# Projection steps spread among the groups of recurrence products, by priority and by TensorE's queue order

## The chip, the cores and the metric

The kernel runs on one core of one Trainium2 chip. The metric is device time in microseconds (us) of one execution: the median of three runs before is 3184.94 us (3180.3 to 3184.98). Queries of the trace give times from the start of the profiled span. TensorE is called PE in them, its weight loads PEld, VectorE DVE, ScalarE ACT, GpSimd POOL, and the queue from which most transfers are issued SP.

## The reference

One layer of a transformer-like block on 1024 latent tokens and 256 context tokens, width 1024, everything in float32: a modulated SwiGLU, then a mixer, then a second SwiGLU and a norm. What matters here is the mixer:

```python
c_q, c_k, c_v, c_g, c_r, c_rk, c_rv, c_gret, c_grw = jnp.split(uc @ w_in, IN_SPLITS, axis=-1)
l_q, l_k, l_v, l_g, l_r, l_rk, l_rv, l_gret, l_grw = jnp.split(ul @ w_in, IN_SPLITS, axis=-1)
...
y_ret_l, _ = retention_segment(axial_rope(hd(l_q), rows, cols), axial_rope(hd(l_k), rows, cols) * k_scale,
                               hd(l_v), log_gamma, ret_state_c)
...
def step(s, inp):                      # rwkv7_scan, two directions, 8 heads of 64
    rt, wt, kt, vt, at, bt = inp
    sa = jnp.einsum('zbhvk,zbhk->zbhv', s, at)
    s_new = s * wt[..., None, :] + sa[..., :, None] * bt[..., None, :] + vt[..., :, None] * kt[..., None, :]
...
rw_out = rwkv_readout(y_rw, r, k, v, xg, g1, g2, r_k, ln_w, ln_b).astype(dt) @ w_rwkv_o
return (jax.nn.sigmoid(gate_ret) * ret_out + jax.nn.sigmoid(gate_rw) * rw_out) @ w_out
```

The recurrence (`rwkv7_scan`) needs only `r`, `k`, `v` and its decays. The columns of `w_in` for the retention (`q`, `k`, `v`, `g`) and for the two gates (`gret`, `grw`) are needed only after it.

## The kernel before, in words

The change lies in one stage, some 950 us long, in which two independent bodies of work share the engines.

*The recurrences* (`Rwkv.recurrences`) go through the tokens in 10 steps. A step takes one pair of 64-token chunks for each of the two directions (z = 0, 1). `prep` loads a pair's operands, scales them, and computes its Gram products `gps` on TensorE (64 rows deep), masked by VectorE into `g`; it also transposes (`btps`, `vtps`) and, for one direction, computes `bops`. `inverse` inverts the triangular parts of `g` in 32x32 blocks on VectorE (`invt`, `invx`, 60 instructions for both directions), with a transposition through DRAM before and after it (SP: `scr<-g`, `invn<-scr`, `scr<-invx`, `g<-scr`). `join` makes 64x64 inverses of the 32x32 ones with the small products `hps` and `xps`. `chain` then applies the pair to the state `S`, once for each chunk: `q` from the state, `q` from the values (`wv`), the correction `u`, the state's update (also named `u` in the trace) and, for latents, the outputs (again `q`). The products of `chain` are 64 by 64, except those from `S`. `readout` normalises finished tokens. `prep` and `inverse` of step s + 2 stand behind `chain` of step s in the program, and the ring of four buffers allows no more.

*The projections* (`Mixer.fill`: `qkvg`, then `gates`) are 72 blocks of 128 columns by up to 512 tokens. `block` splits the block's weights into a high and a low part (`K.cols`: SP loads `wraw`, ScalarE makes `whi`, GpSimd `wlo`) and runs 8 steps of three matmuls each (`mm3`, tile `fps`), 576 steps and 1728 matmuls in all. ScalarE evacuates the bank into `gs`, rotary turns follow for `q` and `k` (SP `rsw`, GpSimd and VectorE), and SP stores the result. Two banks, two weight buffers.

A scheduler orders each engine's queue at build time: it takes ready instructions by priority, which is the place in the program unless the program says otherwise, along its own estimate of time. `fill` is written after `recurrences`, so its instructions have the lowest priority and are put where the estimate has an engine free. On the chip each queue is then executed in that order. A float32 product of the recurrence stands once in the order and twice in the trace.

Of the kernel before, what the change touches and what calls it, by code (L numbers as in the profile page):

```python
# [17 lines left out]
P = 128  # L18
D = 1024
KT = 8  # L20
# [138 lines left out]
class Kern:  # L159
# [44 lines left out]
    def mm3(self, ps, w, ws, x, xs, start, stop, full=None):  # L204
        mm = self.nc.tensor.matmul
        xs = (full, xs) if full else xs
        mm(ps, w[0][:, ws], x[0][xs], start=start, stop=False)  # L207
        mm(ps, w[0][:, ws], x[1][xs], start=False, stop=False)  # L208
        mm(ps, w[1][:, ws], x[0][xs], start=False, stop=stop)  # L209

    def proj(self, ps, w, u, n):
# [315 lines left out]
class Mixer:  # L527
# [222 lines left out]
    def groups(self, which, u, here=False):  # L750

        for c0, n in which:
            for k in range(KT):
                for i in range(2):
                    if not here:
                        self.nc.sync.dma_start(out=u[i][:, k, :n].bitcast(F32), in_=self.dram["u", i][:, k, c0:c0 + n])
            yield c0, n, u
            here = False

    def block(self, u, n, col, pp):  # L760
        ps = pp.tile([P, 512], F32, tag="f", name="fps")[:, :n]
        self.K.proj(ps, self.K.cols(self.a["w_in"][0], col), u, n)
        return ps

    def qkvg(self, u, pool, pp):

        nc, a = self.nc, self.a
        for c0, n, u in self.groups(TURN, u, True):
            lat = c0 < TL
            if lat:  # L770
                cs = {}
                for k in ("cos", "sin"):
                    cs[k] = pool.tile([P, 512], F32, tag=k, name=k, bufs=1)
                    nc.sync.dma_start(out=cs[k], in_=a["cst_" + k][:, c0:c0 + n])
            for hd in range(4):
                for i, nm in enumerate(("q", "rk", "rv", "sg")):
                    if i in (0, 3) and not lat:
                        continue
                    ps = self.block(u, n, 512 * i + hd * P, pp)
                    t = pool.tile([P, 512], F32, tag="gs", name="gs")[:, :n]  # L780
                    if i == 3:
                        nc.scalar.activation(t, ps, AF.Tanh, scale=0.5)
                        nc.vector.scalar_tensor_tensor(out=t, in0=t, scalar=1.0, in1=ps, op0=ALU.add, op1=ALU.mult)
                    else:
                        nc.scalar.activation(t, ps, AF.Copy)
                    if i < 2 and lat:
                        sw = pool.tile([P, 512], F32, tag="rsw", name="rsw", bufs=1)
                        for b in range(0, P, 64):
                            nc.sync.dma_start(out=sw[b:b + 32], in_=t[b + 32:b + 64])
                            nc.sync.dma_start(out=sw[b + 32:b + 64], in_=t[b:b + 32])  # L790
                        nc.gpsimd.tensor_tensor(out=sw, in0=sw, in1=cs["sin"], op=ALU.mult)
                        nc.vector.tensor_tensor(out=t, in0=t, in1=cs["cos"], op=ALU.mult)
                        nc.vector.tensor_tensor(out=t, in0=t, in1=sw, op=ALU.add)
                    nc.sync.dma_start(out=self.dram[nm][hd, :, c0:c0 + n], in_=t)

    def gates(self, u, pool, pp):

        for c0, n, u in self.groups(LAT[::-1], u, True):
            for m0, nm in ((3584, "gret"), (4608, "grw")):
                for m in range(8):  # L800
                    ps = self.block(u, n, m0 + m * P, pp)
                    g = pool.tile([P, 512], F32, tag="gs", name="gs")
                    self.nc.scalar.activation(g, ps, AF.Tanh, scale=0.5)
                    self.nc.sync.dma_start(out=self.dram[nm][m, :, c0:c0 + n], in_=g)

# [45 lines left out]
class Rwkv(Mixer):  # L851
# [16 lines left out]
    def prep(self, s, z, ring, tmp, pp):  # L868
# [73 lines left out]
        bt = ring.tile([P, 4, 2, P], F32, tag="bt", name="bt")  # L942
        for h0 in range(0, 4, 2):
            ps = pp.tile([P, 2, 2, P], F32, tag="mm", name="btps")
# [4 lines left out]
        wv = ring.tile([P, 4, 2, P], F32, tag="wv", name="wv")  # L949
        ps = pp.tile([P, 4, P], F32, tag="mm", name="vtps")  # L950
        for hp in range(4):
# [39 lines left out]
    def join(self, g, tmp, pq):  # L991
# [3 lines left out]
        for e in range(2):  # L995
# [3 lines left out]
            psh, psx = (pq.tile([P, 8, 32], F32, tag="us", name=nm) for nm in ("hps", "xps"))  # L999
            nc.vector.transpose(tt[rf].rearrange("p q t -> p (q t)"), g[rf, e, :, :, rf].rearrange("p a b t -> p (a b) t"))  # L1000
            for q in range(8):
                nc.tensor.matmul(psh[rs, q], gb(rf, q, rs), tt[rf, q], start=True, stop=True, tile_position=(of, os))
            nc.scalar.activation(tt[rs], psh[rs], AF.Copy)
            for q in range(8):
                nc.tensor.matmul(psx[rf, q], tt[rs, q], gb(rs, q, rs), start=True, stop=True, tile_position=(os, of))
            nc.vector.tensor_copy(out=g[rf, e, :, :, rs].rearrange("p a b t -> p (a b) t"), in_=psx[rf])

    def chain(self, un, z, y, first, last, tmp, ps_):
# [8 lines left out]
        for e in (0, 1) if z == 0 else (1, 0):  # L1017
# [3 lines left out]
            for hp in range(4):  # L1021
                mm(q[qr, hp], ar[:, hp, e, ac], S[:, hp], start=hp == 0, stop=False)
            for hp, h in every:
# [4 lines left out]
            for hp, h in every:  # L1028
                mm(us[A, hp, hc[h]], g[A, e, hp, h, A], qa[A, hp, hc[h]], start=True, stop=True)
            nc.scalar.activation(wv[A, :, e], us[A], AF.Copy)  # L1030
            if not (last and e == 1 - z):
                st = us.rearrange("p h v -> p (h v)")[:, :256].rearrange("p (h v) -> p h v", h=4)
                for hp, h in every:
                    mm(st[hc[h], hp], bt[:, hp, e, hc[h]], wv[:, hp, e, hc[h]], start=True, stop=True)
                for h in range(2):
# [3 lines left out]
            if lat:  # L1039
                for hp, h in every:  # L1040
                    mm(q[R, hp, hc[h]], g[:, e, hp, h, R], wv[:, hp, e, hc[h]], start=False, stop=(hp, h) == (3, 1))
                if first:
                    nc.scalar.activation(y[R], f4(q[R]), AF.Copy)
                else:
                    nc.vector.tensor_tensor(out=y[R], in0=y[R], in1=f4(q[R]), op=ALU.add)
# [31 lines left out]
    def recurrences(self, ctx):  # L1077
# [14 lines left out]
        ready(1)  # L1092
        late, joined = [], set()

        def join(i):
# [456 lines left out]
```

## Time and profile before

| | |
|---|---|
| median of 3 runs | 3184.94 us |
| profiled execution | 3190.72 us, span 3188.8 us |
| TensorE busy | 2984.3 us (94%) |
| VectorE, ScalarE, GpSimd busy | 1891.5 (59%), 1041.9 (33%), 958.2 us (30%) |
| mean granted TensorE clock | 0.943 |
| projections (`fps`, L207 to L209), each of three lines | 576 matmuls, 236.4 to 240.6 us busy |

Busy time counts the time in which at least one instruction of an engine is in flight. Matmuls overlap, so their mean duration (some 420 ns for a projection matmul) is longer than the distance of their starts. "Granted clock" is the share of its full clock that TensorE was given; the page prints it in tenths for 40 slices of the span. The row of a stretch holds its borders, its length, then busy time and number of instructions of PE, PEld, DVE, ACT and POOL, then the granted clock, the share of the DMA engines and GB/s; when it is asked for one tile, engines without that tile may be missing.

### The profile page before, as it was taken

The page shows a single profiled execution, that of the slowest core. Times are in us where ns is not written, and L with a number is a line of the kernel's source. Part 1 is how long each engine was busy: PE and PEld are TensorE (multiplying, and loading weights), DVE is VectorE, ACT ScalarE, POOL GpSimd, SP SyncE. Part 2 cuts the span into 40 slices and gives each one's busy share as a digit, 9 for nine tenths or more (in the row PEclk, how much of TensorE's full clock was granted, in tenths as well). Part 3 has the DMA queues.
Part 4 walks back from the last instruction along what each step waited for, and adds up shares of the span by engine and source line. Part 5 has one row for each costly group of instructions (what it writes and reads, how often), then busy time and mean ns, then how long its engine had stood idle before and what let it go on. Part 6 is the DMA issues. An engine that isn't in the chain of part 4 may idle for free.

```text
span 3188.8 us, 45522 instructions
## 1 busy us (share of the span) xinstructions
PE 2984.3 (94%) x17239; PEld 2481.0 (78%) x17239; DVE 1891.5 (59%) x3226; ACT 1041.9 (33%) x1753; POOL 958.2 (30%) x768
## 2 busy tenths in 40 slices
PE   8999999999999999888888899897999799999998
PEld 4888888888887787677776777776778688888877
DVE  4886666544447783676656656754576777665012
ACT  5111111111114465433333334344424533332221
POOL 2111111111113411543333333332215433333542
PEclk9999999999999999887788799998999899999999
DMA  5433222111114446554544454544544344448641
GB/s 212 131 104 93 82 81 77 50 40 40 40 40 166 152 141 213 169 148 137 162 135 114 120 149 128 168 119 147 166 155 137 95 139 140 140 145 302 217 170 60
DMA packets 505747, 416.45 MB, mean 131 GB/s; under 512 B 93464, under 2 KB 402648, under 8 KB 505528
## 3 DMA queue, kind: packets, MB, share of 16 engines
q1 hardware_dynamic: 488976, 401.65, 40.9%
q10 hardware_dynamic: 16552, 11.90, 1.2%
q8 instruction: 136, 2.23, 0.3%
q14 instruction: 83, 0.68, 0.1%
HBM read 309.89 MB, written 99.35 MB: 128 GB/s over the span
## 4 chain that ended last, share of the span: by engine, by line
PE 69%; DVE 13%; DMA 8%; SPq 3%; issue 3%; ACT 2%; POOL 2%; DVEq 0%; ACTq 0%; POOLq 0%
PE psd L207 5%; PE psd L208 5%; PE psd L209 5%; PE p L208 4%; PE p L207 4%; PE p L209 4%; PE psg L209 3%; PE psu L207 3%; PE psu L208 3%; PE psu L209 3%; PE psg L208 3%; PE psg L207 3%; DVE invt L980 2%; DVE invx L981 2%; PE fps L209 1%
## 5 line engine op out<-in xcount | busy, mean ns | idle before, releaser
L197 POOL TENSOR_TENSOR wlo<-wraw,whi 128x512 fp32r<-128x512 f32 (+1 forms) x246 | 442.4, 1811 | 1281.2 <-ACT whi L196 1248.6
L389 DVE SCALAR_TENSOR_TENSOR h<-psd,g,h 128x512 f32<-128x512 f32 (+1 forms) x504 | 313.5, 656 | 272.4 <-PE psd L209 272.1
L196 ACT ACTIVATE whi<-wraw 128x512 fp32r<-128x512 f32 (+1 forms) x246 | 193.9, 804 | 328.9 <-DMA wraw<-in_w_in_dram 72.2
L207 PE MATMUL fps<-uh,whi 128*128 128x512 f32 (+1 forms) x576 | 240.6, 419 | 14.1 <-ACT whi L196 6.7
L207 PE MATMUL p<-v,fac 128*128 128x512 f32 x616 | 241.7, 393 | 11.4 <-ACT v L42 6.3
L209 PE MATMUL fps<-uh,wlo 128*128 128x512 f32 (+1 forms) x576 | 240.2, 418 | 7.5 <-POOL wlo L197 6.8
L208 PE MATMUL p<-v,fac 128*128 128x512 f32 x616 | 241.6, 392 | 4.6 <-DVE v L43 4.6
L209 PE MATMUL p<-v,fac 128*128 128x512 f32 x616 | 241.3, 392 | 0.0
L208 PE MATMUL fps<-ul,whi 128*128 128x512 f32 (+1 forms) x576 | 236.4, 411 | 2.9 <-DMA ul<-d_u 2.9
L207 PE MATMUL psd<-hh,whi 128*128 128x512 f32 (+1 forms) x528 | 189.7, 359 | 4.8 <-DVE h L389 4.6
L207 PE MATMUL psg<-uh,whi 128*128 128x512 f32 (+1 forms) x528 | 188.5, 357 | 0.9 <-ACT whi L196 0.9
L208 PE MATMUL psg<-ul,whi 128*128 128x512 f32 (+1 forms) x528 | 188.8, 358 | 0.4 <-POOL ul L259 0.4
L209 PE MATMUL psg<-uh,wlo 128*128 128x512 f32 (+1 forms) x528 | 188.7, 357 | 0.0
L207 PE MATMUL psu<-uh,whi 128*128 128x512 f32 (+1 forms) x528 | 187.9, 356 | 0.4 <-ACT whi L196 0.4
L208 PE MATMUL psu<-ul,whi 128*128 128x512 f32 (+1 forms) x528 | 187.8, 356 | 0.0
L209 PE MATMUL psu<-uh,wlo 128*128 128x512 f32 (+1 forms) x528 | 187.5, 355 | 0.0
L208 PE MATMUL psd<-hl,whi 128*128 128x512 f32 (+1 forms) x528 | 187.1, 354 | 0.0
L209 PE MATMUL psd<-hh,wlo 128*128 128x512 f32 (+1 forms) x528 | 186.7, 354 | 0.0
L376 ACT ACTIVATE hh<-sg 128x512 fp32r<-128x512 f32 (+1 forms) x66 | 36.9, 559 | 365.4 <-DVE sg L374 308.2
L43 POOL TENSOR_TENSOR fac<-draw,fac 128x512 fp32r<-128x512 f32 x88 | 114.4, 1305 | 138.6 <-ACT fac L42 135.7
L207 PEld LDWEIGHTS fps<-uh,whi 128*128 128x128 f32 x576 | 119.0, 207 | 40.4 <-ACT whi L196 8.9
L209 PEld LDWEIGHTS fps<-uh,wlo 128*128 128x128 f32 x576 | 118.8, 206 | 35.7 <-POOL wlo L197 10.4
(363 smaller groups left out, 7085.2 us busy)
## 6 DMA issues: line engine op xcount, KB each, us to landing
wraw<-in_w_in_dram SPq DMA_DIRECT2D x144, 256.0 KB
modw<-in_w_mod_dram SPq DMA_DIRECT2D x112, 256.0 KB
fraw<-in_ffn_w_gate_dram SPq DMA_DIRECT2D x88, 256.0 KB
hd<-d_hid SPq DMA_DIRECT2D x44, 512.0 KB
draw<-in_ffn_w_down_dram SPq DMA_DIRECT2D x88, 256.0 KB
wraw<-in_ffn_w_gate_dram SPq DMA_DIRECT2D x22, 512.0 KB
wraw<-in_ffn_w_up_dram SPq DMA_DIRECT2D x22, 512.0 KB
wraw<-in_ffn_w_down_dram SPq DMA_DIRECT2D x22, 512.0 KB
```

Of the source, the lines that this page charges most:

```text
L43: eng.tensor_tensor(out=v[1], in0=x, in1=v[0].bitcast(F32), op=ALU.subtract)
L196: nc.scalar.activation(hi[:, s], raw, AF.Copy)
L197: nc.gpsimd.tensor_tensor(out=lo[:, s], in0=raw, in1=hi[:, s].bitcast(F32), op=ALU.subtract)
L207: mm(ps, w[0][:, ws], x[0][xs], start=start, stop=False)
L208: mm(ps, w[0][:, ws], x[1][xs], start=False, stop=False)
L209: mm(ps, w[1][:, ws], x[0][xs], start=False, stop=stop)
L376: nc.scalar.activation(hh, s, AF.Copy)
L389: nc.vector.scalar_tensor_tensor(out=hs, in0=ps, scalar=gates()[v][:, m:m + 1], in1=hs, op0=ALU.mult, op1=ALU.add)
L980: eng.tensor_tensor(out=tv, in0=x[:, :, :m, i:i + 1].to_broadcast([P, 2, m, w]), in1=n[:, :, i:i + 1, i + 1:].to_broadcast([P, 2, m, w]), ...
L981: eng.tensor_tensor(out=x[:, :, :m, i + 1:], in0=x[:, :, :m, i + 1:], in1=tv, op=ALU.add)
```

## The change

While `recurrences` is traced, `mark` notes the priority at each group of recurrence products (and, in `chain`, the group's last product). Projection step j (a counter, 0 to 575) is then given the priority of a mark: the first one of the loop for j below 130, and the mark at the same share of the list for the rest. The block's weights get the priority of 16 steps earlier, reloads of tokens that of 8 steps earlier, and evacuation, rotary turn and store that of the step behind the block. From step 130 on, the first matmul of the three has to follow, in TensorE's queue alone, the linked recurrence product that is four links before its mark.

```diff
--- before.py
+++ after.py
     def mm3(self, ps, w, ws, x, xs, start, stop, full=None):
...
-        mm(ps, w[0][:, ws], x[0][xs], start=start, stop=False)
+        first = mm(ps, w[0][:, ws], x[0][xs], start=start, stop=False)
...
+        return first
...
+    FREE, SLACK, STEPS = 130, 4, 576
+
+    def mark(self, inst=None):
+        if inst is not None:
+            self.links.append(inst.ins.name if hasattr(inst, "ins") else inst.name)
+        self.marks.append((self.tc.cur_priority, len(self.links)))
+
+    def spot(self, ahead=0):
+        j = max(self.step - ahead - self.FREE, 0)
+        return self.marks[self.lead + min(j * (len(self.marks) - self.lead) // (self.STEPS - self.FREE), len(self.marks) - self.lead - 1)]
+
+    def at(self, ahead=0):
+        return self.tc.high_priority(offset=max(self.tc.cur_priority - self.spot(ahead)[0], 0))
+
     def block(self, u, n, col, pp):
         ps = pp.tile([P, 512], F32, tag="f", name="fps")[:, :n]
-        self.K.proj(ps, self.K.cols(self.a["w_in"][0], col), u, n)
+        with self.at(16):
+            w = self.K.cols(self.a["w_in"][0], col)
+        for k in range(KT):
+            with self.at():
+                x = self.K.mm3(ps, w, slice(k * P, (k + 1) * P), u, (slice(None), k, slice(0, n)), k == 0, k == KT - 1)
+            link = self.spot()[1] - 1 - self.SLACK
+            if self.step >= self.FREE and link >= 0:
+                x = getattr(x, "ins", x)
+                self.tc.add_manual_dep(x, self.links[link], mybir.DependencyInfo(mybir.DependencyClass.NoSync, mybir.DependencyReason.DATA), reason="in turn")
+            self.step += 1
         return ps
...
@@ qkvg, gates: evacuation, rotary turn and store of a block
+                    with self.at():
...
@@ groups: reload of the tokens
+                        with self.at(8):
...
@@ prep, join, chain: before each group of gps, btps, vtps, hps, xps
+            self.mark()
@@ chain: after each group of q, u, the state's update, the outputs
+            self.mark(x)
@@ recurrences
+        self.marks, self.links, self.step = [], [], 0
...
+        self.lead = len(self.marks)
```

Line numbers move by 1 to 40, those of the products named below by 30 to 37. In the order of TensorE's queue, at the third join (`hps`, `xps` of step 2) and the chain behind it (tile `btps` transposes for the next step), there stood before, without a projection matmul in between:

```order
L923 MATMUL gps<-ar,bk 128x128 x8
L1002 MATMUL hps<-tt,g 32x32 x8
L1005 MATMUL xps<-g,tt 32x32 x8
L1002 MATMUL hps<-tt,g 32x32 x8
L1005 MATMUL xps<-g,tt 32x32 x8
L1029 MATMUL u<-qa,g 64x64 x8
L1002 MATMUL hps<-tt,g 32x32 x8
L1034 MATMUL u<-wv,bt 64x64 x8
L923 MATMUL gps<-ar,bk 128x128 x4
```

In the new order the end of the same join and the products of the chain behind it stand so:

```order
L1039 MATMUL xps<-g,tt 32x32 x5
L978 MATMUL btps<-ident,bk 128x128 x8
L1039 MATMUL xps<-g,tt 32x32 x3
L1035 MATMUL hps<-tt,g 32x32 x8
L209 MATMUL fps<-uh,wlo 128x512
L1056 MATMUL q<-S_10082,ar 128x128 x2
L207 MATMUL fps<-uh,whi 128x512
L1059 MATMUL q<-wv,g 64x64
L208 MATMUL fps<-ul,whi 128x512
```

Single projection matmuls now stand between the products of the join and of the chain.

In the order of TensorE's queue in a later chain (first direction, from the state's products on), before:

```order
L1022 MATMUL q<-S_10081,ar 128x128
L1034 MATMUL u<-wv,bt 64x64 x8
L1041 MATMUL q<-wv,g 64x64 x8
L1022 MATMUL q<-S_10081,ar 128x128 x3
L1024 MATMUL q<-wv,g 64x64 x8
L207 MATMUL fps<-uh,whi 128x512
```

And in the new order, in a chain of the same direction:

```order
L1056 MATMUL q<-S_10081,ar 128x128 x4
L207 MATMUL fps<-uh,whi 128x512
L1059 MATMUL q<-wv,g 64x64
L208 MATMUL fps<-ul,whi 128x512
L1059 MATMUL q<-wv,g 64x64
L209 MATMUL fps<-uh,wlo 128x512
L1039 MATMUL xps<-g,tt 32x32 x8
```

The chain's own products, before in unbroken groups, are divided by single matmuls of the projections.

In SP's queue, where an inverse's result goes out to DRAM (`scr<-invx`) and comes back into `g`, there stood before:

```order
L987 DMA scr_13298<-invx 256x1x32 x4
L987 DMA scr_13312<-invx 256x1x32 x2
L989 DMA g<-scr_13298 32x8x32 x4
L987 DMA scr_13312<-invx 256x1x32 x2
L939 DMA d_bv_93<-in_r 128x4x128
L972 DMA scr_13855<-g 32x8x32
L989 DMA g<-scr_13312 32x8x32 x4
```

And now:

```order
L1019 DMA scr_13298<-invx 256x1x32 x4
L1019 DMA scr_13312<-invx 256x1x32 x2
L1021 DMA g<-scr_13298 32x8x32 x4
L1019 DMA scr_13312<-invx 256x1x32 x2
L833 DMA d_grw<-gs 128x512
L194 DMA wraw<-in_w_in_dram 128x4x128
L1021 DMA g<-scr_13312 32x8x32 x4
```

A store of a projection's result and a load of weights now stand ahead of the second direction's reload.

More of the change, by code (lines that the diff above doesn't have):

```diff
@@ L779, in qkvg @@
                     ps = self.block(u, n, 512 * i + hd * P, pp)
[L780 to L794, printed above, removed]
+                    with self.at():
+                        t = pool.tile([P, 512], F32, tag="gs", name="gs")[:, :n]
+                        if i == 3:
+                            nc.scalar.activation(t, ps, AF.Tanh, scale=0.5)
+                            nc.vector.scalar_tensor_tensor(out=t, in0=t, scalar=1.0, in1=ps, op0=ALU.add, op1=ALU.mult)
+                        else:
+                            nc.scalar.activation(t, ps, AF.Copy)
+                        if i < 2 and lat:
+                            sw = pool.tile([P, 512], F32, tag="rsw", name="rsw", bufs=1)
+                            for b in range(0, P, 64):
+                                nc.sync.dma_start(out=sw[b:b + 32], in_=t[b + 32:b + 64])
+                                nc.sync.dma_start(out=sw[b + 32:b + 64], in_=t[b:b + 32])
+                            nc.gpsimd.tensor_tensor(out=sw, in0=sw, in1=cs["sin"], op=ALU.mult)
+                            nc.vector.tensor_tensor(out=t, in0=t, in1=cs["cos"], op=ALU.mult)
+                            nc.vector.tensor_tensor(out=t, in0=t, in1=sw, op=ALU.add)
+                        nc.sync.dma_start(out=self.dram[nm][hd, :, c0:c0 + n], in_=t)
     def gates(self, u, pool, pp):
@@ L943, in prep @@
         for h0 in range(0, 4, 2):
+            self.mark()
             ps = pp.tile([P, 2, 2, P], F32, tag="mm", name="btps")
@@ L1003, in join @@
             nc.scalar.activation(tt[rs], psh[rs], AF.Copy)
+            self.mark()
             for q in range(8):
@@ L1021, in chain @@
             for hp in range(4):
-                mm(q[qr, hp], ar[:, hp, e, ac], S[:, hp], start=hp == 0, stop=False)
+                x = mm(q[qr, hp], ar[:, hp, e, ac], S[:, hp], start=hp == 0, stop=False)
+            self.mark(x)
             for hp, h in every:
@@ L1028, in chain @@
             for hp, h in every:
-                mm(us[A, hp, hc[h]], g[A, e, hp, h, A], qa[A, hp, hc[h]], start=True, stop=True)
+                x = mm(us[A, hp, hc[h]], g[A, e, hp, h, A], qa[A, hp, hc[h]], start=True, stop=True)
+            self.mark(x)
             nc.scalar.activation(wv[A, :, e], us[A], AF.Copy)
@@ L1033, in chain @@
                 for hp, h in every:
-                    mm(st[hc[h], hp], bt[:, hp, e, hc[h]], wv[:, hp, e, hc[h]], start=True, stop=True)
+                    x = mm(st[hc[h], hp], bt[:, hp, e, hc[h]], wv[:, hp, e, hc[h]], start=True, stop=True)
+                self.mark(x)
                 for h in range(2):
@@ L1040, in chain @@
                 for hp, h in every:
-                    mm(q[R, hp, hc[h]], g[:, e, hp, h, R], wv[:, hp, e, hc[h]], start=False, stop=(hp, h) == (3, 1))
+                    x = mm(q[R, hp, hc[h]], g[:, e, hp, h, R], wv[:, hp, e, hc[h]], start=False, stop=(hp, h) == (3, 1))
+                self.mark(x)
                 if first:
```

9 lines of the change are left out of this document (6 added, 3 removed).

## The prediction

> **What bounds the kernel now.** I read the page first, then the stage in which recurrences and projections run together, cut by recurrence step, then waits and single products inside it.
>
> ```profile
> span 3188.8 us, 45522 instructions
> PE 2984.3 (94%) x17239; PEld 2481.0 (78%) x17239; DVE 1891.5 (59%) x3226; ACT 1041.9 (33%) x1753; POOL 958.2 (30%) x768
> PEclk9999999999999999887788799998999899999999
> ```
>
> TensorE is busy 94% of the span, and its granted clock dips in slices 17 to 28, about 1260 to 2210 us: this stage. Here it is by recurrence step. The first two rows are the lead (until the first join) and the rest of step 0; each later row ends with the last correction product `u` (L1029) of a step.
>
> ```profile
> core 0: us, PE busy (x) PEld busy (x) DVE busy (x) ACT busy (x) POOL busy (x), PEclk, DMA share, GB/s
> 1259.00:1384.00 125.00, 111.81 (x532) 87.66 (x533) 80.25 (x148) 51.45 (x99) 61.84 (x56) 0.86 0.60 167
> 1384.00:1466.40 82.40, 67.25 (x598) 55.04 (x594) 55.01 (x112) 28.30 (x57) 28.88 (x28) 0.82 0.60 166
> 1466.40:1543.50 77.10, 63.81 (x579) 56.18 (x580) 50.84 (x109) 27.33 (x54) 28.34 (x30) 0.74 0.52 141
> 1543.50:1624.90 81.40, 75.03 (x613) 63.45 (x613) 53.38 (x110) 28.38 (x55) 28.74 (x30) 0.82 0.50 141
> 1624.90:1712.30 87.40, 75.33 (x659) 61.82 (x659) 57.71 (x114) 32.53 (x61) 31.92 (x31) 0.90 0.43 120
> 1712.30:1802.40 90.10, 72.06 (x608) 59.94 (x608) 57.35 (x116) 29.70 (x57) 29.52 (x29) 0.79 0.42 113
> 1802.40:1890.80 88.40, 81.25 (x666) 68.36 (x666) 50.23 (x108) 36.24 (x70) 30.77 (x34) 0.81 0.52 141
> 1890.80:1980.30 89.50, 84.93 (x712) 70.47 (x711) 55.09 (x123) 37.87 (x71) 30.30 (x32) 0.94 0.51 143
> 1980.30:2064.90 84.60, 73.91 (x627) 60.42 (x627) 58.10 (x128) 28.39 (x49) 35.79 (x33) 0.90 0.59 173
> 2064.90:2150.70 85.80, 78.21 (x679) 64.96 (x678) 52.44 (x129) 33.07 (x58) 31.97 (x29) 0.94 0.44 120
> 2150.70:2207.80 57.10, 48.80 (x432) 41.31 (x431) 20.12 (x53) 22.01 (x40) 15.65 (x13) 0.88 0.37 118
> ```
>
> The rows cover 949 us. Summing length times one minus clock gives 17.5 + 14.8 + 20.0 + 14.7 + 8.7 + 18.9 + 16.8 + 5.4 + 8.5 + 5.1 + 6.9 = 137 us of lost clock. TensorE is busy in 88% of it (832 of 949), so 120 us of its time are stretching. Vector work fills 62%.
>
> Three matmuls make one projection step; I call them a triple. In the order before, the steps of these rows hold (from step 1) 43, 44, 49, 32, 45, 67, 53, 57 and 34 triples. The step with 32 took 90.1 us, the one with 67 took 89.5. So a triple is mostly hidden behind the recurrence's own round trips: the **path share** of a us of TensorE work lies between 0 and 1. Between steps 6 and 7 it is (89.5 - 84.6) over the difference in full-clock work, 84.93 x 0.94 - 73.91 x 0.90 = 13.3: 0.37. I take 0.35 for ordinary work.
>
> Where does the clock go? Three stretches, first all work, then the tile `fps` (projections) alone:
>
> ```profile
> 1460.80:1484.50 23.70, 22.01 (x191) 19.75 (x192) 8.23 (x20) 9.71 (x20) 8.17 (x8) 0.50 0.56 143
> 1529.10:1563.10 34.00, 28.61 (x252) 24.95 (x253) 12.88 (x23) 12.12 (x26) 7.25 (x8) 0.50 0.71 199
> 1563.20:1597.20 34.00, 28.91 (x264) 23.88 (x262) 31.82 (x64) 12.83 (x23) 15.74 (x16) 1.00 0.34 100
> ```
>
> ```profile
> 1529.10:1563.10 34.00, 4.15 (x8) 2.49 (x9) 0.00 (x0) 0.00 (x0) 0.50 0.71 199
> 1631.40:1645.00 13.60, 6.71 (x14) 4.30 (x14) 0.00 (x0) 0.60 (x1) 0.50 0.40 126
> 1870.40:1945.30 74.90, 42.93 (x173) 31.37 (x172) 0.00 (x0) 4.14 (x7) 1.00 0.54 147
> ```
>
> For 34 us the clock was 0.50 although TensorE was busy for 28.6: almost all of it small recurrence products, 4.15 us of projections. VectorE had 12.9 us of work there and waited. With projections at 57% (42.93 of 74.90) the clock held at 1.00. So dense runs of small products without projections go with the half clock, and in them the round trip waits for TensorE itself: there I give a us saved a path share of 0.65, nearer to 28.6/34 than to 0.35.
>
> The Trainium skill ("TensorE: Matmul & The Clock Gate", Part 1) puts the half clock down to idle: after an idle window of some 3.4 us. The trace disagrees: 22.01 of 23.70 us busy at 0.50. By that rule this change would win no clock, since it removes no long wait; that is the second case below.
>
> **The change, part by part.** Prices of single products, from the timeline of TensorE (start, duration):
>
> ```profile
> 1849.21 0.39 PE L209 MATMUL fps<-uh,wlo 128*128 128x512 f32 x1
> 1849.44 0.39 PE L207 MATMUL fps<-uh,whi 128*128 128x512 f32 x1
> 1849.76 0.69 PE L1034 MATMUL u<-wv,bt 128*64 128x64 f32 x16
> ...
> 1924.89 0.50 PE L207 MATMUL fps<-uh,whi 128*128 128x512 f32 x1
> 1925.22 0.40 PE L208 MATMUL fps<-ul,whi 128*128 128x512 f32 x1
> 1925.46 0.39 PE L209 MATMUL fps<-uh,wlo 128*128 128x512 f32 x1
> ...
> 1562.39 0.63 PE L208 MATMUL fps<-ul,whi 128*128 128x512 f32 x1
> 1562.82 0.54 PE L209 MATMUL fps<-uh,wlo 128*128 128x512 f32 x1
> ```
>
> By starts, a projection matmul takes 0.23 us at full clock and 0.43 at half, so a triple is 0.69. Before a small product it takes 0.32, and as the first after small ones 0.33: each change of array shape costs about 0.1 us that these rows show, and perhaps as much again at its other edge.
>
> No instruction is added or removed; 1728 projection matmuls and all recurrence products stay. Terms, against the profiled execution (3190.72 us, 1.9 over its span and 5.8 over the median of 3184.94):
>
> 1. Lead. Up to step 0's last `u` the new order has 136 triples, the old 152; up to the first join product 89 against 106.
>
> ```profile
> 1300.00:1340.00 40.00, 37.29 (x197) 29.27 (x195) 16.78 (x29) 19.69 (x37) 20.31 (x19) 1.00 0.64 179
> ```
>
> TensorE is busy 37.3 of 40 us where the first Gram products wait behind projections, so the 16 fewer triples count in full: 16 x 0.69 = -11 us (0 if the first inverse is late for another reason).
>
> 2. Step 1 gets 84 triples for 43: 41 x 0.69 = 28 us of work, at 0.35: +10 (0 to +28).
>
> 3. Steps 2 to 7 get 304 for 290: 9.7 us of work, +3 (0 to +10).
>
> 4. Steps 8 and 9 get 52 for 91: 27 us less, -9 (0 to -27).
>
> 5. Shape changes. From the first projection to just after the last, neighbours of different array shape go from 388 to 575. 187 more at 0.1 to 0.2 us, say 0.15, are 28 us of work, at 0.35: +10 (+0 to +37). The Trainium skill ("TensorEngine Tiling (Array Packing)", Key Properties) says that a change of tiling mode drains the engine; it gives no price, and speaks against this change as the rows do.
>
> 6. Clock. Unbroken runs of 32 or more recurrence products between two projections fall from 20 (1016 products) to 14 (695), by 32%. If the stretched time falls alike, 0.32 x 120 = 38 us of TensorE work go, at 0.65: -25 us (0 to -80, the latter if two thirds of the 120 go at full share).
>
> 7. SP's queue. Loads of weights and stores of results move with the steps. Between the first store of an inverse's result and its last reload, where the old order has projection transfers in one step of ten, the new one has one or two in eight of ten, five times with one that waits for ScalarE's `gs`.
>
> ```profile
> SPq L804 <- ACT gs L803: 86.1, 22, 11.5
> ```
>
> Such a wait is 3.9 us in the mean; five are 20 us. The second half of a join stands behind each, and part of the time its queue would have waited anyway: +7 (0 to +20). On POOL the low-half splits stay between the state decays as before, and ScalarE's evacuations move with their products; the same count at nearby places, 0 (-5 to +5, by the 6.8 us row below).
>
> What does not change is the waits of TensorE on the recurrence itself; they are late next if the clock gets better:
>
> ```profile
> PE q L1022 <- DVE y L1045: 16.5, 5, 5.5
> PE hps L1002 <- DVE tt L1000: 10.8, 4, 4.6
> PE q L1022 <- DVE S L1038: 8.8, 5, 5.9
> PE fps L209 <- POOL wlo L197: 6.8, 8, 1.9
> ```
>
> Sum: -11 + 10 + 3 - 9 + 10 - 25 + 7 = -15. 3190.7 - 15 = 3175.7 for a profiled run, so 3170 against the median.
>
> **The rivals.** The clock decides between them; the other six terms add to +10.
>
> *Clock better, faster* (the forecast): from 3105 (term 6 at its end and term 5 at 0, 65 us under the forecast) to 3178. For it: the full clock at 57% projections, 0.94 in the rows with 57 and 67 triples against 0.74 with 43. Against it: those warm steps took 85.8 and 89.5 us, no less than the cold ones with 77.1 and 81.4.
>
> *No clock gained*: the half clock follows waits, and the waits above remain. Then +10 stands alone, or near 0 with shares near 0: 3179 to 3195, within or just over the bound. For it, the flat step times; against it, 28.6 busy us at 0.50. The clock gate page of the Trainium skill would have it so.
>
> *Clock worse, slower*: projections in short runs hold a warm clock, but don't bring a cold one back. In 1631 to 1645 they were half of the stretch (6.71 of 13.60) and it stayed at 0.50, while the old order's long runs, which end cold stretches, are cut: runs of 12 matmuls or more fall from 66 to 53. If the mean of the stage falls from 0.86 to 0.81, 0.05 x 949 x 0.88 x 0.65 = 27 us come on top of +10: 3185 + 37 = 3222. It is over 0.2% (6.4 us, about what a measurement of this kernel can tell from no change) as soon as the clock gains less than some 6 us on the path.
>
> That the order does not spread at all can be put aside for short runs (134 runs of projections become 237), though by step it is no more even than before: 18 to 84 against 32 to 67.
>
> **Numbers.** Chances: clock better 0.52, none gained 0.20, worse 0.28. The first gives faster by over 0.2% nearly always (0.50); the second splits, 0.13 within and 0.07 slower; the third is slower but for 0.03. So faster 0.50, same 0.16, slower 0.34. Predicted 3170 us. Range 3105 to 3216: below lies a clock near 1.00 throughout (0.08), above the worse half of the third case (0.12). The first case's own range is 3105 to 3178.
>
> **What would show it.** Right: cut by step, clock at 0.90 or more in steps 1 to 5 where it was 0.74 to 0.90, step 1 some 10 us longer, steps 8 and 9 shorter, the first join near 1373 us for 1384. Wrong: half-clock stretches of 14 us or more with a third or more of projections in them (lock-in); SP's waits for `gs` just ahead of `g<-scr`, with joins waiting for `tt` over 5 us (term 7 in full); a warm stage with steps still at 85 to 90 us (path share near 0).

## The result, and the profile after

The changed kernel takes 3216.43 us in the median of four runs (3205.88 to 3221.15); the kernel before, on the same chip, 3184.96. The ratio is 1.0097, with a 95% interval of 1.007 to 1.0124: about 1% slower. A second set of four runs (e5 below) gave 1.0063 (1.0041 to 1.0085). The prediction said 15 us faster.

The page of the changed kernel, whose profiled execution took 3217.97 us (span, busy time, clock in 40 slices):

```profile
span 3216.0 us, 45541 instructions
PE 3021.4 (94%) x17239; PEld 2495.6 (78%) x17239; DVE 1896.0 (59%) x3226; ACT 1041.1 (32%) x1754; POOL 960.9 (30%) x768
PEclk9999999999999998877998889877999899999999
```

TensorE is busy 37 us longer with the same 17239 matmuls, and the dip of the clock is still there, now in slices 16 to 28. The stage cut as before, at the first join and then at the last `u` of each step:

```profile
core 0: us, PE busy (x) PEld busy (x) DVE busy (x) ACT busy (x) POOL busy (x), PEclk, DMA share, GB/s
1259.00:1379.90 120.90, 100.56 (x473) 80.11 (x473) 78.55 (x143) 48.78 (x95) 54.53 (x50) 0.84 0.57 164
1379.90:1469.50 89.60, 84.22 (x593) 67.72 (x592) 54.48 (x116) 25.82 (x50) 30.43 (x28) 0.71 0.48 132
1469.50:1567.00 97.50, 90.71 (x719) 75.77 (x720) 58.59 (x113) 41.66 (x82) 44.83 (x43) 0.88 0.69 199
1567.00:1651.20 84.20, 77.57 (x639) 61.33 (x639) 50.69 (x112) 29.67 (x56) 37.97 (x34) 0.96 0.47 133
1651.20:1735.40 84.20, 73.59 (x652) 60.30 (x652) 59.62 (x119) 30.76 (x59) 28.25 (x32) 0.89 0.44 123
1735.40:1821.30 85.90, 81.68 (x652) 65.91 (x653) 53.01 (x109) 32.73 (x64) 34.06 (x32) 0.90 0.53 144
1821.30:1918.40 97.10, 91.37 (x676) 72.88 (x676) 48.96 (x108) 34.38 (x67) 28.14 (x30) 0.82 0.41 113
1918.40:2005.90 87.50, 79.52 (x673) 65.17 (x672) 56.49 (x122) 34.31 (x64) 34.21 (x36) 0.88 0.62 177
2005.90:2103.40 97.50, 84.35 (x688) 67.46 (x687) 62.63 (x138) 35.07 (x63) 34.13 (x30) 0.87 0.46 122
2103.40:2176.80 73.40, 63.72 (x555) 51.79 (x555) 48.96 (x118) 24.15 (x42) 22.35 (x21) 0.80 0.31 84
2176.80:2227.50 50.70, 41.74 (x375) 33.98 (x374) 13.77 (x33) 11.14 (x18) 9.05 (x8) 0.77 0.19 55
```

Length times one minus clock sums to 145 us, against 137 before: no clock was gained. The difference of the two traces lies in four stretches: lead and steps 0 and 1, steps 2 to 7, steps 8 and 9, and the tail, which is what I call the time from the last `u` to the first output product `ops` of the retention. First the kernel before, then the changed one:

```profile
1259.40:1543.50 284.10, 242.86 (x1703) 198.86 (x1704) 185.71 (x367) 106.75 (x209) 118.89 (x113) 0.82 0.58 160
1543.50:2064.90 521.40, 462.51 (x3882) 384.46 (x3882) 331.86 (x694) 193.10 (x362) 187.04 (x189) 0.86 0.49 138
2064.90:2207.80 142.90, 127.01 (x1109) 106.28 (x1108) 72.55 (x181) 55.08 (x98) 47.62 (x42) 0.92 0.41 120
2207.80:2387.30 179.50, 158.05 (x911) 135.98 (x911) 120.76 (x324) 64.55 (x108) 41.03 (x21) 0.94 0.52 164
```

```profile
1259.40:1567.00 307.60, 275.08 (x1782) 223.39 (x1782) 191.27 (x368) 115.99 (x226) 129.79 (x121) 0.81 0.58 166
1567.00:2103.40 536.40, 488.09 (x3975) 393.05 (x3975) 331.41 (x703) 196.92 (x372) 196.76 (x193) 0.88 0.49 135
2103.40:2227.50 124.10, 105.46 (x928) 85.77 (x928) 62.73 (x150) 35.29 (x60) 31.40 (x29) 0.79 0.26 72
2227.50:2415.10 187.60, 160.37 (x921) 138.94 (x921) 126.05 (x343) 72.30 (x122) 41.16 (x22) 0.90 0.53 173
```

+23.5, +15.0, -18.8 and +8.1 us: together +27.8, which is the difference of the spans (27.2). The last one was in no term. Length times clock is the same in both tails (179.5 x 0.94 and 187.6 x 0.90, each 169 us), so these 8 us are lost clock. At the end of the recurrences the timeline of the changed kernel shows what happens there (the last projection matmul, the first loads of the retention's first head, its first product):

```profile
2224.89 0.51 PE L209 MATMUL fps<-uh,wlo 128*128 128x512 f32 x1
2225.46 0.32 SPq L1248 DMA_DIRECT2D rq<-d_q  x1
...
2234.43 0.32 SPq L1246 DMA_DIRECT2D rvt<-d_rv  x1
...
2238.55 2.37 PE L1254 MATMUL vps<-ident,rvt 128*128 128x128 f32 x10 [9.18 <-DMA rvt<-d_rv]
```

and of SP's waits:

```profile
SPq L1248 <- PE fps L209: 26.0, 1, 26.0
SPq L833 <- ACT gs L832: 109.6, 16, 19.5
```

SP's queue stood 26 us at the retention's first load until the last projection was done, and TensorE then waited 9.18 us for the next load; from 2230.8 to 2254.7 us its clock was 0.50. The waits on `gs` rose from 86.1 to 109.6 us.

**How the runs are compared.** Each run gives a span and a mean granted clock. I call span times clock the warm work and the rest the lost clock, and take means over the runs. Over 31 runs of the kernel before warm work is 3004.4 us (standard deviation 4.6), lost clock 184.4 (5.5). The two are not independent: in these runs 1 us more of lost clock went with 0.5 us less warm work, so that it came to about half a us of time. Shape changes are counted here between full-array and part-array products within the stage: 288 before, 456 after (the prediction's 388 and 575 take every change of tile); for e6 and e7 the table has the changes that the edit adds. Ratios are to the kernel before on the same chip, where its median lies between 3185 and 3192 us.

| kernel | median us | ratio [95%] | shape changes | warm work | lost clock |
|---|---|---|---|---|---|
| before (31 runs) | 3191.05 | | 288 | 3004.4 | 184.4 |
| changed (4 runs) | 3216.43 | 1.0097 [1.007, 1.0124] | 456 | 3023.5 | 189.6 |
| e5 changed again | 3208.59 | 1.0063 [1.0041, 1.0085] | 456 | 3023.2 | 182.8 |
| e1 early | 3190.43 | 0.9992 [0.997, 1.0015] | 530 | 3033.3 | 154.0 |
| e2 blocks of 8 | 3193.43 | 1.0011 [0.9994, 1.0029] | 360 | 3015.5 | 176.5 |
| e3 blocks of 32 | 3196.43 | 1.0014 [0.9999, 1.003] | 318 | 2999.6 | 193.9 |
| e4 products alone | 3183.34 | 0.9972 [0.9955, 0.9989] | 436 | 3012.6 | 166.9 |
| e6 alternating | 3200.45 | 1.004 [1.0026, 1.0054] | +432 | 3045.9 | 154.9 |
| e7 grouped | 3179.77 | 0.9977 [0.9957, 0.9997] | +144 | 3021.0 | 159.0 |
| e8 products alone, early | 3154.4 | 0.9894 [0.9879, 0.9909] | 474 | 3016.6 | 135.5 |
| e9 loads as written | 3180.3 | 0.9979 [0.9963, 0.9995] | 420 | 3019.6 | 159.9 |
| e10 stores as written | 3222.34 | 1.0105 [1.0078, 1.0132] | 460 | 3033.8 | 186.8 |
| e11 e8 in blocks of 8 | 3161.8 | 0.9918 [0.9896, 0.9939] | 338 | 3006.8 | 152.4 |
| e12 no links | 3162.1 | 0.9922 [0.9892, 0.9952] | 430 | 3002.7 | 158.0 |
| e13 links to step 460 | 3179.4 | 0.996 [0.9939, 0.9982] | 426 | 3016.1 | 160.1 |
| e14 e8 without links | 3175.15 | 0.9939 [0.9914, 0.9964] | 472 | 3019.2 | 152.9 |
| e15 e12 early | 3185.34 | 0.9977 [0.9955, 1.0] | 430 | 3018.9 | 165.3 |

### The profile page after: what moved, and what is told of

It reads as the page before. It is cut to its first block, busy times and chain, and to the rows that moved or that the text cites. A ratio compares the mean times of both kernels' runs of the same rounds, so it can differ in the third digit from the quotient of the medians.

```text
span 3216.0 us, 45541 instructions
## 1 busy us (share of the span) xinstructions
PE 3021.4 (94%) x17239; PEld 2495.6 (78%) x17239; DVE 1896.0 (59%) x3226; ACT 1041.1 (32%) x1754; POOL 960.9 (30%) x768
## 4 chain that ended last, share of the span: by engine, by line
PE 70%; DVE 13%; DMA 8%; issue 3%; SPq 2%; ACT 2%; POOL 1%; DVEq 0%; ACTq 0%; POOLq 0%
PE psd L207 5%; PE psd L208 5%; PE psd L209 5%; PE p L207 4%; PE p L208 4%; PE p L209 4%; PE psg L209 3%; PE psu L208 3%; PE psu L209 3%; PE psu L207 3%; PE psg L207 3%; PE psg L208 3%; DVE invx L1013 2%; DVE invt L1012 2%; PE fps L207 2%
## 5 line engine op out<-in xcount | busy, mean ns | idle before, releaser
L207 PE MATMUL fps<-uh,whi 128*128 128x512 f32 (+1 forms) x576 | 248.7, 436 | 9.6 <-ACT whi L196 3.1
L207 PEld LDWEIGHTS p<-v,fac 128*128 128x128 f32 x616 | 117.0, 190 | 35.9 <-ACT v L42 6.4
```

What stands on the lines that cost most here:

```text
L207: first = mm(ps, w[0][:, ws], x[0][xs], start=start, stop=False)
```

## The experiments

The theories at the start: (1) the added shape changes are the loss; (2) the tail is, since late projections hold up the retention; (3) lost clock goes with runs of products without projections. Later ones have letters and are told with the run that tests them. Unless said otherwise a diff is against the changed kernel. The expectations number projection steps 0 to 575 and recurrence steps 0 to 9; where those of e1 to e3 speak of half steps 4, 6 and 8, the counts are those at the ends of recurrence steps 3, 5 and 7.

**e1, e2, e3: an earlier end; fewer shape changes.**

```diff
 e1
-    FREE, SLACK, STEPS = 130, 4, 576
+    FREE, SLACK, STEPS = 130, 4, 700
 e2 (e3 with 32 for 8)
-        j = max(self.step - ahead - self.FREE, 0)
+        j = max((self.step - ahead) // 8 * 8 - self.FREE, 0)
```

> The changed kernel with STEPS 700 in place of 576: the same projections at earlier marks, so that the last of the 576 steps stands at the end of half step 8 of the recurrences on TensorE instead of after the last one. Shape changes 530 (456 in the changed kernel, 288 before). Theory 1, the added shape changes are the loss, each 0.15 to 0.19 us and nearly all of it on the path: 74 more of them, 3225 to 3232 us. Theory 2, the tail: retention's loads wait for buffers that the late projections hold, 14 us between the last u and the first ktps (0 before); here that wait is gone: 3200 to 3205 if it is all, about 3213 if theory 1 holds beside it. Theory 3, the clock: runs of 32 and more products without a projection fall from 14 to 4; if they cost what the prediction said, lost clock falls from 145 us to below 110 and the time to about 3190.

Measured 3190.43 us. Warm work is the highest of the spread kernels so far (3033), as its 530 shape changes would have it, and lost clock falls by 30 us against before and 36 against the first four runs of the changed kernel. That is the time of theory 3, about 3190, and nearly its lost clock; but warm work rose by 10 us beside it, as theory 1 says, so the number alone does not decide for theory 3.

> The changed kernel with the mark looked up once for every 8 steps (a block) and not for each step: the same spread over the recurrences (320, 430, 517 triples by half steps 4, 6, 8; changed kernel 320, 425, 524), but 360 shape changes in place of 456. Theory 1 (shape changes): 96 fewer at 0.15 to 0.19 us, 14 to 18 us less: about 3200. Theory 2 (tail): the projections end where they did, so about 3216. Theory 3 (clock): runs without projections as before the change (17 with 1054 products), lost clock not below 145 us and the time 3216 or more.

> As e2, the mark looked up once for 32 steps: 318 shape changes, spread 320, 432, 523 triples by half steps 4, 6, 8, and 1377 products in runs of 32 and more without a projection (695 in the changed kernel, 1016 before). Theory 1 (shape changes): 138 fewer, 21 to 26 us less: about 3193. Theory 2 (tail): 3216. Theory 3 (clock): longer runs without projections lose more clock, 3225 to 3240.

Measured 3193.43 and 3196.43. Warm work falls with the shape changes, by 24 us against the changed kernel in e3, as theory 1 says (21 to 26), and by 8 in e2, half of what it says. The clock does not answer to the count of products in runs without projections alone: e2, with 1054, lost 176 us, the changed kernel, with 695, 186.

One place explains some of this. At the end of step 0 the changed kernel and e2 have the same 216 products in the same order, and TensorE is hardly idle in them; changed kernel, then e2:

```profile
1440.80:1469.50 28.70, 28.30 (x216) 25.17 (x215) 12.72 (x34) 5.50 (x10) 4.97 (x7) 0.50 0.39 101
```

```profile
1437.60:1455.50 17.90, 17.90 (x216) 15.87 (x216) 11.40 (x31) 5.51 (x10) 4.95 (x7) 0.88 0.48 112
```

28.7 us at half clock, 17.9 at 0.88. The changed kernel stays at 0.50 for the 47.5 us around it:

```profile
1435.50:1483.00 47.50, 45.44 (x333) 40.18 (x334) 19.94 (x43) 11.02 (x21) 13.81 (x14) 0.50 0.50 139
1435.50:1483.00 47.50, 14.74 (x57) 12.75 (x58) 0.64 (x1) 1.36 (x3) 0.50 0.50 139
```

The second row is the tile `fps` alone: 31% of the stretch is projections, TensorE is busy in 45.44 of 47.50 us, and the clock does not come back. That is just under the third which the prediction named as the sign of lock-in, its third rival. Three other half-clock stretches of this trace are over it: 17.0 us from 1374.1 (64% projections), 27.3 us from 1824.6 (38%, with TensorE busy throughout) and 17.0 us from 2097.7 (40%). The kernel before has three over a third, each of 13.4 to 13.6 us. So the sign is there.

The order of the products alone does not set it. e13 below has the changed kernel's order on TensorE up to step 460, and in its trace the clock is at half here for 17 us, not 47.5. And e12, far faster, has a half-clock stretch of 41.0 us from 1430.3. Each of these is one trace.

**e4: products alone spread.** All `with self.at(8)`, `at(16)` and `at()` around transfers, evacuations and stores become `if True`; the one around `mm3` stays.

> The changed kernel with the spreading for the projections' products alone: weights, reloads of u, evacuations and stores stay at the priority of the place where they are written. 436 shape changes. Theory 1 (shape changes): 20 fewer, 3212 to 3216. Theory 4 (SP's queue: stores of gs issued early stand ahead of the loads of g, 109.6 us of waiting on gs against 86.1): without the early stores the waits of g are as before and 8 to 15 us go: 3201 to 3208. Against it: evacuations that come late hold the PSUM buffers of the next block, 3220 or more.

Measured 3183.34, faster than before and under every range expected. With nearly as many shape changes (436) as the changed kernel, it cannot be they that separate the two: most is lost clock (167 against 186), some warm work. That the stores are the cause, theory 4, is put to the test by e9 and e10.

**e5: the changed kernel again.** No edit.

> The changed kernel itself, on the chip of e1 to e4 or its like. The span of each run, times its mean granted clock, is called warm work here, and the rest of the span the lost clock; before the change (31 runs) they are 3004 and 184 us, in the four runs of the changed kernel 3023 and 190. If both hold, the median is again 3205 to 3220, with warm work 3019 to 3027. If the long half-clock stretch of its trace (47.8 us from 1435.5; e2 ran the same products in the same order there at full clock from 1441.8) is a matter of the single run, lost clock is 165 to 190 and the time 3190 to 3205.

Warm work 3023.2 and a ratio of 1.0063: the first reading holds. The half-clock stretch is in its trace too (41.0 us from 1429.3).

**e6, e7: the price of a shape change.** Against the kernel before:

```diff
-        self.K.proj(ps, self.K.cols(self.a["w_in"][0], col), u, n)
+        w = self.K.cols(self.a["w_in"][0], col)
+        for m in (64, 128, 64, 128, 64, 128):        # e7: (64, 64, 64, 128, 128, 128)
+            self.nc.tensor.matmul(ps[:m, :64], w[0][:m, :m], u[0][:m, 0, :64], start=True, stop=True)
+        self.K.proj(ps, w, u, n)
```

> The kernel before, with six products of 64 columns added ahead of each of the 72 blocks' own (they are overwritten): a 64x64 one and a 128x128 one in turn, so six shape changes in each block, 432. To be read against e7, which issues the same 432 products with two changes in each block. Theory 1 (each change costs 0.15 to 0.19 us of TensorE, nearly all of it on the path): 288 changes, 43 to 55 us longer than e7. With the prediction's path share of 0.35: 15 to 19 us longer. The runs so far (warm work against shape changes, 3004 at 288, 3033 at 530) say 0.12 us of time for each: 35 us.

> As e6 with the three 64x64 products first and then the three of 128x128: two shape changes in each block. 432 small products at 0.06 to 0.15 us, on the path by 0.35 to 1: 9 to 65 us over the kernel before; the difference to e6 is what is asked.

e6 is 20.7 us longer than e7 in the median; warm work differs by 24.9 us: 24.9 / 288 = 0.086 us for each change. This price is rough, for the two do not differ in the changes alone. The added products also moved the scheduler's order: by the end of step 3 the traces hold 256 projection steps in e6, 278 in e7 and 288 in the kernel before, and some of the groups of six are divided. The timeline shows the price on TensorE itself, e6 and then e7, where all six products stand together:

```profile
1917.51 1.26 PE L764 MATMUL fps<-uh,whi 64*64 64x64 f32 x6
1918.61 0.47 PE L207 MATMUL fps<-uh,whi 128*128 128x512 f32 x1
```

```profile
1906.56 0.81 PE L764 MATMUL fps<-uh,whi 64*64 64x64 f32 x6
1907.20 0.48 PE L207 MATMUL fps<-uh,whi 128*128 128x512 f32 x1
```

From the first of the six to the product behind them it is 1.10 us against 0.64: 0.46 us for four changes more, 0.115 each. By these two figures the path share is about 0.75 (0.086 / 0.115), not 0.35. e7 was expected 9 to 65 us over the kernel before and is 9 us under it, with 432 products more: 17 us more warm work and 24 us less lost clock. Whether the products or the moved order (93 projection steps ahead of the first join, 106 in the kernel before) spared the clock, this run does not show.

**e8: products alone, early.** e4 with STEPS 640.

> e4 (products alone spread) with STEPS 640: the last of 576 steps stands at the end of step 7 of 0 to 9; 474 shape changes (e4 436), 523 products in runs of 32 and more without a projection (e4 879). Theory 1: 38 more changes, warm work 5 to 7 us over e4's 3013. Theory 3 (clock, as e1 showed with lost clock 154 against 184): lost clock 150 to 160 in place of 167. Sum 3175 to 3185, so 0.2 to 0.5% under the kernel before. Rival: the two steps without projections lose what the others gain, 3185 to 3200.

3154.4 us: 1.1% under the kernel before, 1.7% under the changed one on the same chip (e5), and 21 us under the low end expected. Lost clock is 135.5 and not 150 to 160. Its four stretches:

```profile
1259.40:1534.00 274.60, 241.09 (x1713) 195.52 (x1713) 181.09 (x364) 107.70 (x209) 119.22 (x114) 0.87 0.60 171
1534.00:2089.30 555.30, 524.10 (x4167) 418.09 (x4166) 335.06 (x707) 214.36 (x400) 217.42 (x211) 0.94 0.51 142
2089.30:2222.20 132.90, 110.68 (x1154) 101.44 (x1153) 98.56 (x311) 63.21 (x115) 28.21 (x25) 0.83 0.36 110
2222.20:2356.60 134.40, 116.51 (x573) 97.21 (x574) 85.96 (x186) 34.71 (x53) 33.59 (x17) 0.92 0.56 179
```

Against the changed kernel: -33.0 at the beginning, +18.9 in steps 2 to 7, which carry 372 projection steps in place of 304, +8.8 in steps 8 and 9, and -53.2 in the tail. The projections end in step 7, so the retention's first loads and products run beside steps 8 and 9 (1154 matmuls there, without one projection, for 928).

**e9, e10: which of the moved parts costs.** e9: `at(8)` and `at(16)` become `if True`. e10: the two `with self.at():` in `qkvg` and `gates` do.

> The changed kernel with weights and reloads of u at the priority of the place where they are written; products, evacuations and stores spread as in the change. 164 triples before step 0's last u (136 in the changed kernel, 152 before), 48 in step 1 (84 and 43), 420 shape changes. Theory A (warm work follows the shape changes, 0.086 us of time each by e6 against e7): 132 more than before, 3016 us warm. Theory B (the stretch of 41 to 48 us at half clock that ends step 0 comes with the lead cut to 136 triples): it is gone, lost clock as in e4, 167, and the time about 3185. If the loss is not tied to the lead, lost clock 183 to 190 and 3200 to 3206.

> The changed kernel with evacuations and stores at the priority of the place where they are written; products, weights and reloads spread. 162 triples before step 0's last u, 69 in step 1, 460 shape changes. Theory A: 172 more changes than before, 3019 us warm. Theory B: lost clock 165 to 175, and 3187 to 3196. If early loads of weights are what costs, lost clock and time are those of the changed kernel, 3200 to 3210.

3180.3 and 3222.34. With e4 and the changed kernel this is a square of ratios:

| | stores as written | stores spread |
|---|---|---|
| loads as written | 0.9972 (e4) | 0.9979 (e9) |
| loads 16 and 8 steps early | 1.0105 (e10) | 1.0097, 1.0063 (changed) |

With the links in place, issuing weights and reloads early costs 0.8 to 1.3%, whatever the stores do; early stores cost nothing that shows. Theory B falls in its form: e10's lead is not cut (162 projection steps) and it loses the most. Theory A misses there too: e10's warm work is 3033.8 us, 15 over the 3019 expected. In the traces, one of each, the cost lies at the beginning, in lead and steps 0 and 1; e9, then e10:

```profile
1259.40:1542.80 283.40, 246.08 (x1740) 199.84 (x1741) 190.12 (x367) 110.65 (x214) 124.26 (x117) 0.87 0.60 170
```

```profile
1259.40:1595.60 336.20, 281.85 (x1814) 226.00 (x1813) 194.96 (x375) 120.22 (x233) 136.79 (x125) 0.81 0.55 159
```

e10 takes 52.8 us more there for 19 projection steps more (231 against 212, some 13 us). At 0.81 for 0.87 it loses 64 us of clock for 37. Within these bounds TensorE's longest wait in it is that of the joins for their transposed input, 18.9 us, in e9 the 7.4 of the same row:

```profile
PE hps L1035 <- DVE tt L1032: 18.9, 4, 9.4
```

**e11: e8 with fewer shape changes.** e8 with the edit of e2.

> e8 with the mark looked up once for 8 steps: nearly the same triples by the end of each step (204, 284, 357, 416 at the ends of steps 1 to 4; e8 204, 278, 343, 399), 338 shape changes in place of 474, 955 products in runs of 32 and more without a projection in place of 523. Theory A: 136 fewer changes, 12 us less warm work, 3005. Theory 3 (clock by runs without projections): lost clock 150 to 165 in place of 135. Sum 3157 to 3172, slower than e8; if the clock does not follow those runs, 3142.

3161.8: as theory A and theory 3 said together. 136 changes fewer, 9.8 us less warm work (0.072 each), and 17 us more lost clock. The two effects nearly cancel: 0.9918 against 0.9894, with intervals that overlap.

**e12, e13: the links, and the tail alone.**

```diff
-            if self.step >= self.FREE and link >= 0:
+            if False:                                                  # e12
+            if 460 > self.step >= self.FREE and link >= 0:             # e13
```

> The changed kernel without the added links in TensorE's queue order, priorities alone. Lead and step 1 are the same (136 and 84 triples), 430 shape changes, the last projection in step 8 and not after it. Theory A: 26 fewer changes, 2 us less; theory B: the stretch at half clock stays; the tail (14 us from the last u to the first ktps) goes: 3195 to 3206. If the links' waits are the loss: under 3195.

3162.1 us, with lead and step 1 as in the changed kernel. That is far under the 3195 to 3206 expected, and under 3195 is where the expectation put it if the links' waits are the loss. Theory A misses by 18 us of warm work (3002.7, and about 3021 by its count). Steps 8, 9 and tail:

```profile
2099.70:2235.10 135.40, 120.03 (x1188) 108.59 (x1187) 97.71 (x313) 63.98 (x118) 28.71 (x25) 0.84 0.38 112
2235.10:2372.80 137.70, 119.80 (x572) 99.76 (x573) 86.70 (x187) 34.95 (x54) 33.77 (x17) 0.91 0.56 177
```

The tail falls from 187.6 to 137.7 us, steps 8 and 9 take 11 more; together this is 39 of the 42 us by which the four stretches are shorter. I had put the tail at 14 us, the gap before the first product, when the whole of the retention's first part can move into steps 8 and 9.

> The changed kernel with the added links only up to step 460 (the middle of step 6 of 0 to 9); the last 116 steps have priorities alone. Queue order up to there as in the changed kernel; 576 triples by the end of step 8 as in e12 (after step 9 in the changed kernel), 426 shape changes. Theory C (the links hold the last projections until the recurrences end, and retention, whose loads wait for their buffers, starts late: 186 to 188 us from the last u to the first ops in the changed kernel, 138 in e12): the tail is 135 to 145 us and the median 3160 to 3175. If the links cost all along the stage (SP's waits on gs are 110 and 106 us in the changed kernel, 64 in e12), the tail gives half or less, 3185 to 3200.

3179.4, between the two readings. Queue order up to step 460 is that of the changed kernel; freeing the last 116 steps gives 33 of e12's 49 us (mean spans 3209.5, 3176.2, 3160.8). Lead to step 1, then steps 8 and 9 and the tail in its trace:

```profile
1259.40:1554.80 295.40, 263.42 (x1782) 213.38 (x1781) 190.06 (x370) 115.76 (x226) 131.97 (x121) 0.85 0.61 173
...
2084.10:2207.30 123.20, 110.92 (x1045) 96.10 (x1044) 72.82 (x194) 51.49 (x94) 32.63 (x30) 0.85 0.35 101
2207.30:2370.80 163.50, 144.82 (x806) 124.21 (x806) 117.21 (x304) 52.24 (x85) 38.86 (x20) 0.94 0.55 171
```

Its last projection ends at 2144 us, 63 before the last `u`; in e12 it is 110, in e8 135. The tail is 24 us shorter than in the changed kernel; another 12 us lie in the beginning, with the same products (x1782) at a clock of 0.85 for 0.81, which the links behind it cannot have brought. Steps 2 to 7 give 7 more. The tail alone gives half of e12's 50 us, where the second reading had half or less, and its 24 us are about half of what this trace gains. So the tail is a large part of what the links cost in the changed kernel, nearly all of it in e12 and half in e13; the rest is not settled.

**e14, e15: without links, early.** e14: e8 with `if False` as in e12. e15: e12 with STEPS 640.

> e8 without the added links. Projections end in step 8 and not step 7 (571 triples by the end of step 7; e8 576), 472 shape changes (474). Theory C: both end before the recurrences do, so the tail is 130 to 140 us as in e8 and the time that of e8, 3148 to 3162. If links cost all along the stage: 3130 to 3148.

> e12 with STEPS 640: 576 triples by the end of step 7 of 0 to 9 (e12 563), lead and step 1 as in the changed kernel (136, 84), 430 shape changes, 400 products in runs of 32 and more without a projection (e12 695). Against e14 it has the weights, reloads, evacuations and stores spread too. Theory C: tail 130 to 138, 3152 to 3165; the clock as in e8 (135 us lost): 3145. If the lead cut short costs 10 us of clock at the end of step 0: 10 over e14.

Both miss the times that theory C gave. e14 takes 3175.15; by ratios that is 14 us over e8, which ran on another chip, and it is nearly all lost clock (152.9 for 135.5). Here, where the projections end early anyway, the order with links was the better one. e15 takes 3185.34, with a range of 35 us over ten runs. That is 10 us over e14, with 12 us more lost clock and the same warm work, which is what the expectation's last reading named. Warm work is 16 us over e12's with the same number of shape changes. Its profiled run (span 3164.5) is its fastest, so its trace cannot say where; this stays open. Both end the projections early and have short tails in their traces (133 and 131 us), yet neither reaches e8, e11 or e12.

## Why the prediction was wrong

The profiled execution was 27 us longer where 15 less were forecast. Warm work rose by 19 us and the lost clock stayed (186 in the mean of eight runs, 184 before). The step that failed is term 6, the clock, together with a term that was missing, the tail.

- *Term 6, clock, -25.* Measured +2, in the rows of the trace +8. The stretched time was taken to follow the runs of 32 products without a projection. It does not follow them alone: e12 has the same 695 products in such runs and loses 158 us, 28 less, while e11 with longer runs than e8 did lose 17 more. Most of the 25 us were to be had, but with loads, links or the end of the spread set otherwise (e1, e4, e9, e12 and e13 lose 154 to 167, before 184). The third rival, lock-in, shows its sign (27.3 us at half clock with 38% projections), but that its 3222 us is near the result is luck: its 27 us of clock did not come; warm work did. What sets the clock stays open: e13 ran the changed kernel's order with 17 us at half clock where the changed kernel had 47.5.
- *No term for the tail.* The prediction followed each step to the last `u` and stopped. The trace of before showed 179.5 us from there to the first `ops`; the change holds the last projections until the recurrences end, the retention's loads wait behind them (26.0 us on SP), +8 us. Where projections end early, in e8 and e12, this tail is 50 us shorter and steps 8 and 9 are 9 to 11 us longer: more than any term of the prediction.
- *Term 5, shape changes, +10.* By 0.086 us and 168 changes 14 us, within its range; the cost per change was sized too high (0.15, measured 0.115), the path share far too low (0.35, measured 0.75). By this price it would be most of the 19 us of warm work; no run shows it apart, and e12 with 430 changes has 2 us less warm work than the kernel before with 288.
- *Term 2, step 1, +10.* Measured +20.4, or 0.73 of the 28 us of added work. At full clock, 97.5 x 0.88 = 85.8 against 77.1 x 0.74 = 57.1: 28.7 us, all of it. So the path share is 0.7 to 1 there. The 0.37 took the work of its two rows at full clock but their lengths as they came; with both at full clock they give (89.5 x 0.94 - 84.6 x 0.90) / 13.3 = 0.60. This share is the second step that failed.
- *Term 1, lead, -11.* Measured +3.1 to the end of step 0. At full clock it is right: 120.9 x 0.84 + 89.6 x 0.71 = 165.2 against 125.0 x 0.86 + 82.4 x 0.82 = 175.1, -9.9. Lost clock took 13 us back, 45 us in these rows for 32. The first join came at 1379.9, not 1373.
- *Terms 3 and 4.* Steps 2 to 7 +15.0 for +3, with their part of the shape changes; steps 8 and 9 -18.8 for -9, again at more than 0.35 of the 27 us.
- *Term 7, SP's queue, +7.* The waits on `gs` came (109.6 us), but the joins did not wait longer for `tt` (7.6 us against 10.8), and e9 against e4 shows no cost of early stores. What costs about 1%, with the links in place, is the early loads, which the term put in one sum with the stores. How they take the clock is not settled: e10's joins wait longer, but no run moved one load alone.

Two sums of the prediction are off besides, and change nothing in the forecast. The third rival passes 0.2% once the clock gains less than 3.6 us (10 less 6.4), not some 6. And the 0.02 that the first case leaves over went to slower, where its own range, up to 3178, puts it with same.

The Trainium skill ("TensorE: Matmul & The Clock Gate", Part 1) ties the half clock to an idle window. Again the trace disagrees: 28.30 of 28.70 us busy at 0.50. The same section says that the number of cold matmuls varies from run to run, since the window runs freely. Its counts for one kernel, 6 to 14 matmuls, are far under the 216 products above, and no run here shows the window.

## What to carry to other kernels

Follow a change of order to the next stage: work spread up to the end of its cover holds the buffers that the next stage loads into, and in the three fastest kernels it ended early (e8, e11 and e12: at 86 to 89% of the cover). An early end is not enough by itself: e1, e14 and e15 have it and take 3190, 3175 and 3185 us. Price a change of array shape on TensorE well above a third of its cost where it is busy nine tenths of the time (about three quarters here), and split each run into warm work and lost clock before judging an order, since an order can gain in one what it loses in the other. Move one kind of instruction at a time: products spread alone gained, and their loads spread with them, with the links in place, lost more than that.

## What the runs showed of the hardware

- 432 added products of 64 columns, grouped, made the kernel 0.23% faster (0.9977, 0.9957 to 0.9997): 17 us of work against 24 us of clock. The order of the queue moved with them, so the gain cannot be put to the products alone.
- Changes between 64x64 and 128x128 products took 0.115 us of TensorE each (e6 and e7). By warm work a change of shape is 0.07 to 0.09 us (e8 and e11, e2, e6 and e7) and once 0.17 (e3), with the order moving beside it.
- TensorE stayed at half clock while busy in 28.30 of 28.70 us, on products that in another kernel, in the same order, ran at 0.88.
- Executions of one kernel differ in lost clock at least as much as in warm work: standard deviations of 5.5 and 4.6 us for the kernel before, of 10.3 and 5.0 with e2.
